# Row factors of a norm sent round through DRAM instead of transposed, and two small edits in a two-layer trunk

## Chip, cores, metric

One core of one Trainium2 chip. The metric is the device time in microseconds (us) of one execution of the whole program; less is better.

## What is computed

The program is a trunk of two layers for one sequence of 512 tokens and 1024 features, all in float32. Layer 0 has a gated linear attention as its mixer, layer 1 a sparse attention (compressed, selected and window keys) whose keys and values, shared, are projected from the normed residual stream. Each layer adds attention to a memory and a feed-forward part with a convolution of width 3. A norm of all rows ends it.

```python
def rmsnorm(x, g):
    y = x * lax.rsqrt(jnp.mean(x * x, axis=-1, keepdims=True) + EPS)
    return y * g

h = x
for i in range(DEPTH):                                  # DEPTH = 2
    if i == N_A_LAYERS:                                 # before layer 1
        shared = shared_kv(h, kv_norm, w_kv_shared, ...)   # rmsnorm(h, kv_norm) @ w_kv, then compressed keys
    xn = rmsnorm(h, norm_mix[i])
    mem_kv = rmsnorm(mem, norm_mem[i]) @ w_mem_kv[i]
    ...                                                 # main = gla_mixer(...) in layer 0, nsa_mixer(...) in layer 1
    mo = mem_attention(mq, mem_kv)
    h = h + jnp.concatenate([main, mo], axis=-1) @ w_out[i]
    h = h + conv_ffn(rmsnorm(h, norm_ffn[i]), w_up[i], conv_w[i], conv_b[i], w_down[i])
return rmsnorm(h, final_norm)
```

## The kernel before

The residual stream is held transposed, as eight tiles `h[k]` of 128 features by 512 tokens. Every float32 product is made from three matmuls of halves: ACT writes the high half of an operand, rounded to the type float32r, DVE subtracts it to get the low half (`split_to`, `wget`), and TensorE adds high x high, low x high, high x low. Weights come as 512 KB tiles `wraw` from DRAM, issued by SP.

A framework schedules the instructions and sets the semaphores; each engine then runs its own list in order. The helper `after(a, b)` fixes that `a` stands behind `b` in an engine's list or in the schedule without a semaphore. Tiles with a tag share a fixed number of buffers, so a new tile waits for the last reader of the old one.

The change touches three places.

*The norm of layer 1's mixer.* A norm is applied late: the products are made with the unnormed stream and their results are multiplied by one factor per token. `rms_sums` adds up the squares with matmuls against a column of ones; the result `rc` has tokens on the partitions (128 x 4), DVE scales it, and POOL raises it to the power -1/2. But the products here have features on the partitions and tokens along the row, so the factors are needed in each partition, as `rb` (128 x 512). `rms_rows` does that with four transposes of a broadcast column (L351, TensorE) into a bank of PSUM and one copy by ACT (L353). In `nsa_layer` the loop over the eight feature tiles makes the product with the compressed keys' and values' weights (L1566, into four banks `pk`); at its step 3 it calls `rms_sums`, at step 5 `rms_rows`. After the loop come the gates' products (L1571), then `kf = pk[f] * rb` on DVE (L1575), which empties the banks for the next keys (L1605). Sixteen copies on SP's queue stack `kf` into `T` (L1578, L1579); DVE adds positions to it (`tp`, L1653) and TensorE multiplies that (L1666).

*The last steps of the sparse attention.* Twelve steps (`steps`, six pairs of heads, two sets of query tiles each) run as a pipeline: scores of the next step (`scores`, with L1761 on DVE, L1763 on ACT, L1768 and L1771 on POOL), transposes of this step's weights (`weights_t`: TensorE L1706, then copies PT by ACT or DVE, L1873), products with the values of an earlier one (`values`). After steps 8, 9 and 10 the outputs `o[0]`, `o[1]`, `o[2]` of the first three pairs are split into halves for the output product `w_out` (L942); PcT is the transposed weights of the compressed part (copy L1805).

*The last rows of the program.* In `ffn_seven` the function `end` finishes two of four blocks of 128 tokens behind the last matmuls; here tokens are on the partitions. `closing` adds the last product to the rows (`plus`, L1378), takes the sum of their squares on ACT (L1383) and multiplies them by the final gain on DVE (L1384). `factor` (L1387, DVE) scales that sum and adds the part known earlier (`pre`), `rooted` (L1391, POOL) raises it to -1/2, `closed` (L1397, L1399) multiplies the rows and sends them out.

Of the kernel before, what the change touches and what calls it, by code (L numbers as in the profile page):

```python
# [12 lines left out]
F32 = mybir.dt.float32  # L13
FR = mybir.dt.float32r
AF = mybir.ActivationFunctionType
ALU = mybir.AluOpType
AX = mybir.AxisListType

S = 512
D = 1024  # L20
# [154 lines left out]
class Trunk:  # L175
# [102 lines left out]
    def split_to(self, hi, lo, src, scale=None):  # L278

        nc = self.nc  # L280
        if scale is None:
            self.high_ins = nc.scalar.activation(hi, src, AF.Copy)  # L282
            nc.vector.tensor_tensor(out=lo, in0=src, in1=hi.bitcast(F32), op=ALU.subtract)  # L283
        else:
            self.high_ins = nc.scalar.activation(hi, src, AF.Copy, scale=scale)
            nc.vector.scalar_tensor_tensor(out=lo, in0=src, scalar=scale, in1=hi.bitcast(F32), op0=ALU.mult, op1=ALU.subtract)
# [60 lines left out]
    def rms_rows(self, N, tag):  # L347

        pb = self.ps("pt")
        for t in range(N // 128):  # L350
            self.nc.tensor.transpose(pb[:, 128 * t:128 * t + 128], self.rc[:, t:t + 1].to_broadcast([128, 128]), self.ident)  # L351
        self.rb = self.t(self.tmp if not tag else self.mpool, [128, N], "rb" + tag, bufs=1)
        self.nc.scalar.copy(self.rb, pb[:, :N])  # L353

    def rms_at(self, first, second, N=S, tag=""):
        return {first: lambda: self.rms_sums(N, tag), second: lambda: self.rms_rows(N, tag)}
# [858 lines left out]
    def ffn_seven(self, l):  # L1215


        nc, tc, T = self.nc, self.tc, NJ // 2
# [108 lines left out]
        def end(mms):  # L1327
# [52 lines left out]
            def closing(t, c, a, bank=None):  # L1380
                plus(t, c, banks[2][t] if bank is None else bank)
                jk = self.t(self.tmp, [128, 512], "rb", bufs=1)
                nc.scalar.activation(jk[:, c], y[t][0][:, c], AF.Square, accum_out=a)  # L1383
                dve(nc.vector.tensor_tensor(out=z[t][:, c], in0=y[t][0][:, c], in1=gb[0][:, c], op=ALU.mult))  # L1384

            def factor(t, a, r):
# [25 lines left out]
            plus(1, cs[1], banks[2][1])  # L1412
            closed(0)
            factor(1, ss[:, 5, 0:1], pre[:, 1:2])
            closing(1, cs[1], ss[:, 1, 0:1], own)
            factor(1, ss[:, 1, 0:1], rc[:, 1:2])
            rooted(1)
            closed(1)

# [93 lines left out]
    def nsa_layer(self):  # L1513
        nc, I, tc = self.nc, self.I, self.tc
        GKV, GMIX = 6, 1
        with ExitStack() as outer:
# [17 lines left out]
            with tc.tile_pool(name="nsap", bufs=2) as pp:  # L1534
# [19 lines left out]
                for n, k in enumerate(order):  # L1554
                    if n % 2 == 0:
                        wh, wl = self.wget(self.W["kvc"][k // 2], GKV, (k, k + 1))
                    if n == 3:
                        self.rms_sums(S, "")
                    if n == 5:
                        self.rms_rows(S, "")  # L1560
                        gate_weights()
                    xh, xl = self.x[k]
                    for f in range(4):
                        ws = slice(512 * (k % 2) + 128 * f, 512 * (k % 2) + 128 * f + 128)
                        for i, (u, w_) in enumerate(((wh, xh), (wl, xh), (wh, xl))):
                            nc.tensor.matmul(pk[f], u[:, ws], w_, start=n + i == 0, stop=n == 7 and i == 2)  # L1566
# [207 lines left out]
            def compressed(a):  # L1774
# [27 lines left out]
                pt = self.ps("pt")  # L1802
                for u in range(2):
                    tr(pt[:, 128 * u:128 * u + 128], Pc[:, 2 * u:2 * u + 2], self.ident)
                nc.scalar.copy(PcTs[a % 2], pt[:, :256].rearrange("p (u t) -> p u t", u=2))  # L1805
                yield

            run = lambda g, n=1: [next(g, None) for _ in range(n)]
# [46 lines left out]
            with tc.tile_pool(name="nsac", bufs=2) as cp:  # L1855
# [3 lines left out]
                def weights_t(s):  # L1859

                    a, qts = steps[s]
                    for hh in range(2):
                        for qt in qts:
                            n = 128 * (qt + 1)
                            P = Ps.pop((a, qt, hh))
                            PT = PTs[a, qt, hh] = self.t(cp, [128, 2, n], f"PT{qt}")
                            for brs in ((0, 1),) if qt < 2 else ((0,), (1,)):
                                pt = self.ps("acc" if brs == (1,) and s < 8 else "pt")
                                for j, br in enumerate(brs):
                                    for kt in range(qt + 1):  # L1870
                                        tr(pt[:, n * j + 128 * kt:n * j + 128 * kt + 128], P[:, br, 128 * kt:128 * kt + 128], self.ident)
                                eng = nc.vector.tensor_copy if qt == 1 or qt == 3 and brs[0] else nc.scalar.copy
                                ins = eng(PT[:, brs[0]:brs[-1] + 1, :], pt[:, :n * len(brs)].rearrange("p (b k) -> p b k", b=len(brs)))  # L1873
                                if qt != 1 and not (qt == 3 and brs[0]):
                                    turned[s] = ins
                                yield

                def values(*ss):
# [25 lines left out]
                for s, (a, qts) in enumerate(steps):  # L1904
# [7 lines left out]
                    for i in range(6):  # L1912
# [13 lines left out]
                        if i == 0 and s < 11:  # L1926
                            run(before, 4)
                        run(now)
                        run(proj, 2)
                        if qts[0] == 0 and i in (0, 5):  # L1930
                            run(c)
                        if i == 2 and s == 11:
                            run(before, 2)
                    if 8 <= s < 11:
                        main[s - 8] = self.split(o[s - 8], self.xp, [128, S], "x")
                run(values(11), 2)
            self.w_out(1, main)
# [26 lines left out]
```

## Time and profile before

| | us |
|---|---|
| median of 3 runs | 1230.78 |
| lowest, highest | 1229.76, 1231.19 |
| profiled execution, whole | 1230.46 |
| its span, first to last instruction | 1228.6 |

In the profile PE is TensorE's matmul, PEld its loading of weights (which overlaps), DVE VectorE, ACT ScalarE, POOL GpSimd and SP SyncE, the engine that issues most DMAs. L12 is line 12 of the kernel. A row of the timeline has start (us from the span's start), length, engine, line, operation, out<-in by tile names, the count of merged instructions, and in brackets the idle time before it with what ended it. A row that ends in two or more merged instructions gives the length of all of them. Matmuls overlap, so the distance between their starts tells more than their length. A row of an instruction's group has its shortest, median and longest duration in ns. In the table of DMAs the last number is us from issue to landing; a queue's row has packets, MB, and the share that its packets took of 16 DMA engines over the span. In a row by stretch come the bounds, the length, the busy time of PE, PEld, DVE, ACT and POOL, the granted TensorE clock (1.00 is full), the DMA engines' busy share and GB/s.

### The profile page before, as it was taken

To read this page: it belongs to the slowest core of one execution; us is meant where nothing else is said; L and a number is where in the kernel's file an instruction comes from. 1 tells how busy PE (TensorE), PEld (TensorE's weight loads), DVE (VectorE), ACT (ScalarE), POOL (GpSimd) and SP (SyncE) were. 2 spreads that over 40 slices of the span, in tenths; PEclk is the share of its full clock that TensorE was granted. 3 is DMA by queue.
4 is the path that set the end of the run, shared out by engine and by line. 5 is a ranking of instruction groups with operands and counts; after the bars stand their busy time and mean duration, and the time that the engine had idled before them with its cause. 6 is when DMAs were issued, how large, how long until landed. Compare 5 with 4: busy or idle time off the path is not lost.

```text
span 1228.6 us, 19292 instructions
## 1 busy us (share of the span) xinstructions
PE 1219.9 (99%) x7189; PEld 1037.3 (84%) x7189; DVE 929.3 (76%) x1714; ACT 667.1 (54%) x1276; POOL 131.1 (11%) x179
## 2 busy tenths in 40 slices
PE   9999999999999999999999999999999999999997
PEld 7888888888888888899888788888888888888886
DVE  7775887599777767878768677974698777777785
ACT  7666555455444444456535777773555444444564
POOL 1000121000000000000103265660000000000000
PEclk9999999999999999999999999999999999999999
DMA  7422111324343343453736333312234334343533
GB/s 260 125 90 77 53 37 46 120 81 150 121 130 112 120 136 105 139 166 99 216 114 205 87 82 95 112 40 69 86 120 138 119 120 133 109 137 120 165 110 112
DMA packets 49594, 142.94 MB, mean 116 GB/s; under 512 B 5679, under 2 KB 9296, under 8 KB 49500
## 3 DMA queue, kind: packets, MB, share of 16 engines
q1 hardware_dynamic: 47692, 139.19, 36.8%
q10 hardware_dynamic: 1808, 2.51, 0.7%
q8 instruction: 57, 0.93, 0.3%
q14 instruction: 37, 0.30, 0.1%
HBM read 133.77 MB, written 2.15 MB: 111 GB/s over the span
## 4 chain that ended last, share of the span: by engine, by line
PE 96%; DVE 1%; ACT 1%; DMA 0%; issue 0%; POOL 0%; SPq 0%; ACTq 0%; POOLq 0%; DVEq 0%
PE acc L979 38%; PE acc L942 5%; PE acc L304 4%; PE acc L693 4%; PE po L1705 3%; PE po L322 3%; PE acc L1705 3%; PE po L1040 3%; PE sc L1040 3%; PE acc L1040 3%; PE sc L1236 2%; PE po L1236 2%; PE acc L1236 2%; PE acc L322 2%; PE sc L304 2%; PE pt L1706 2%
## 5 line engine op out<-in xcount | busy, mean ns | idle before, releaser
L979 PE MATMUL acc<-xh,wl 128*128 128x512 f32 x688 | 267.9, 389 | 0.0
L979 PE MATMUL acc<-xh,wh 128*128 128x512 f32 x688 | 267.8, 389 | 0.0
L979 PE MATMUL acc<-xl,wh 128*128 128x512 f32 x688 | 267.6, 389 | 0.0
L268 ACT ACTIVATE wh<-wraw 128x1024 fp32r<-128x1024 f32 x138 | 145.7, 1056 | 95.8 <-PE acc L942 30.0
L269 DVE TENSOR_TENSOR wl<-wraw,wh 128x1024 fp32r<-128x1024 f32 x138 | 171.7, 1244 | 23.5 <-ACT wh L268 22.8
L979 PEld LDWEIGHTS acc<-xl,wh 128*128 128x128 f32 x688 | 129.1, 188 | 26.9
L979 PEld LDWEIGHTS acc<-xh,wh 128*128 128x128 f32 x688 | 129.2, 188 | 26.4
L979 PEld LDWEIGHTS acc<-xh,wl 128*128 128x128 f32 x688 | 129.1, 188 | 26.1
L965 DVE SCALAR_TENSOR_TENSOR hc<-acc,h,hc 128x511 f32<-128x511 f32 (+1 forms) x144 | 107.3, 747 | 54.4 <-ACT hc L963 53.1
L963 ACT ACTIVATE hc<-acc,h 128x512 f32<-128x512 f32 x72 | 56.0, 777 | 116.8 <-PE acc L979 116.7
L283 DVE TENSOR_TENSOR wl<-wraw,wh 128x1024 fp32r<-128x1024 f32 (+3 forms) x61 | 69.2, 1139 | 16.3 <-ACT wh L282 16.1
L282 ACT ACTIVATE wh<-wraw 128x1024 fp32r<-128x1024 f32 (+3 forms) x61 | 59.0, 970 | 26.7 <-DMA wraw<-in_wp 8.4
L1771 POOL TENSOR_TENSOR P<-P,ssm 128x256 f32<-128x256 f32 (+3 forms) x48 | 63.4, 1343 | 1.9
L1763 ACT ACTIVATE P<-P,smn 128x128 f32<-128x128 f32 (+3 forms) x96 | 53.3, 557 | 10.1 <-DVE smn L1761 8.4
L1761 DVE CUSTOM_DVE_ANT_0 P<-sc,strip 128x128 f32<-128x128 f32 (+3 forms) x72 | 30.0, 434 | 9.5 <-PE sc L1705 9.3
L1525 POOL MEMSET kcz<- 128x128 f32 x1 | 0.2, 210 | 341.7 <-PE acc L1040 341.7
L1025 DVE TENSOR_TENSOR wraw<-wraw,wraw 128x512 f32<-128x512 f32 x22 | 15.1, 688 | 28.4 <-DMA wraw<-in_wp 28.4
L1292 POOL TENSOR_TENSOR yrc<-yrc,mhalf 128x2 f32<-128x2 f32 x1 | 0.7, 698 | 330.0 <-DVE yrc L1291 330.0
L1449 ACT ACTIVATE hc<-hc 128x512 f32<-128x512 f32 x22 | 13.9, 633 | 34.3 <-DVE hc L965 34.1
L1705 PE MATMUL po<-PT,V 128*64 128x128 f32 x480 | 30.3, 273 | 0.0
L1706 PE MATMUL pt<-ident,P 128*128 128x128 f32 x184 | 29.5, 275 | 0.1
L360 DVE TENSOR_TENSOR h<-acc,h 128x512 f32<-128x512 f32 x14 | 9.7, 690 | 25.8 <-PE acc L942 20.5
(594 smaller groups left out, 3140.9 us busy)
## 6 DMA issues: line engine op xcount, KB each, us to landing
wraw<-in_wp SPq DMA_DIRECT2D x227, 512.0 KB, 3.7
strip<-vecd SPq DMA_DIRECT2D x12, 448.0 KB, 3.5
qd<-qf SPq DMA_DIRECT2D x24, 128.0 KB, 2.7
wraw<-in_wp SPq DMA_DIRECT2D x8, 256.0 KB, 3.5
mt<-in_memT SPq DMA_DIRECT2D x16, 128.0 KB, 3.1
h<-in_xp SPq DMA_DIRECT2D x2, 512.0 KB, 6.1
T<-kf SPq DMA_DIRECT2D x8, 128.0 KB, 2.3
T<-kf SPq DMA_DIRECT2D x8, 127.8 KB, 2.4
```

The source lines that it names most:

```text
L268: self.split_ins = nc.scalar.activation(wh, raw, AF.Copy)
L269: self.low_ins = nc.vector.tensor_tensor(out=wl, in0=raw, in1=wh.bitcast(F32), op=ALU.subtract)
L283: nc.vector.tensor_tensor(out=lo, in0=src, in1=hi.bitcast(F32), op=ALU.subtract)
L304: self.nc.tensor.matmul(ps[:M, :N], u[:, M * k:M * k + M], x[k][i][:, :N], start=n == 0, stop=n == 23)
L322: nc.tensor.matmul(ps[:, :N], s_, m_, start=k == 0 and n == 0, stop=k == KC - 1 and n == 2)
L942: nc.tensor.matmul(banks[m], a[:, o], b, start=k == 6 and i == 0, stop=k == 5 and i == 2)
L965: nc.vector.scalar_tensor_tensor(out=dst[:, i:], in0=u[:, :S - i], scalar=tap(2 - i), in1=dst[:, i:], op0=ALU.mult, op1=ALU.add)
L979: pe(nc.tensor.matmul(pu[half], a[:, o], self.x[k][b], start=k == 0 and n == 0, stop=k == KC - 1 and n == 2))
L1040: pe(nc.tensor.matmul(dst, a[:, o], b, start=first and n == 0 and i % 2 == 0, stop=stop and n == 2, skip_group_check=True))
L1236: pe(nc.tensor.matmul(bank[i][:, c], a[:, ts], b[:, c], start=first and n == 0, stop=stop and n == 2, skip_group_check=True))
L1705: mm = lambda *args, **kw: pe(nc.tensor.matmul(*args, **kw))
L1771: nc.gpsimd.tensor_tensor(out=P, in0=P, in1=f[:, i, :].unsqueeze(2).to_broadcast([128, 2, 128 * t + 128]), op=ALU.mult)
```

## The change

`rms_spread` takes the place of `rms_sums` and `rms_rows` for the norm of layer 1's mixer: the 128 x 4 factors are written to DRAM as one row of 512 (512 pieces of 4 bytes), then read back into all 128 partitions. Both DMAs are issued by POOL. The other edits move the split of `o[2]` into step 11 with a fixed place, and let DVE take the last sum of squares, its scale and the addition of `pre` in one instruction, written straight into `rc`.

```diff
+    def rms_spread(self, eng):
+
+        self.rms_sums(S, "")
+        d = self.t(self.dram, [S // 128, 128], "rcd")
+        eng.dma_start(d.rearrange("t p -> p t"), self.rc)
+        self.rb = self.t(self.tmp, [128, S], "rb", bufs=1)
+        eng.dma_start(self.rb, bass.AP(tensor=d.tensor, offset=d.offset, ap=[[0, 128], [1, S]]))
...
             def closing(t, c, a, bank=None):
                 plus(t, c, banks[2][t] if bank is None else bank)
                 jk = self.t(self.tmp, [128, 512], "rb", bufs=1)
-                nc.scalar.activation(jk[:, c], y[t][0][:, c], AF.Square, accum_out=a)
+                if bank is None:
+                    nc.scalar.activation(jk[:, c], y[t][0][:, c], AF.Square, accum_out=a)
+                else:
+                    dve(nc.vector.tensor_tensor_reduce(out=jk[:, c], in0=y[t][0][:, c], in1=y[t][0][:, c], scale=1.0 / D, scalar=pre[:, 1:2],
+                                                       op0=ALU.mult, op1=ALU.add, accum_out=a))
                 dve(nc.vector.tensor_tensor(out=z[t][:, c], in0=y[t][0][:, c], in1=gb[0][:, c], op=ALU.mult))
...
             factor(1, ss[:, 5, 0:1], pre[:, 1:2])
-            closing(1, cs[1], ss[:, 1, 0:1], own)
-            factor(1, ss[:, 1, 0:1], rc[:, 1:2])
+            closing(1, cs[1], rc[:, 1:2], own)
             rooted(1)
...
                     if n == 3:
-                        self.rms_sums(S, "")
+                        self.rms_spread(nc.gpsimd)
                     if n == 5:
-                        self.rms_rows(S, "")
                         gate_weights()
...
-                nc.scalar.copy(PcTs[a % 2], pt[:, :256].rearrange("p (u t) -> p u t", u=2))
+                turned[13] = nc.scalar.copy(PcTs[a % 2], pt[:, :256].rearrange("p (u t) -> p u t", u=2))
...
                                     turned[s] = ins
+                                elif s == 11:
+                                    turned.setdefault(12, ins)
...
                         run(now)
+                        if s == 11 and i == 0:
+                            main[2] = self.split(o[2], self.xp, [128, S], "x")
+                            after(self.high_ins, turned[13])
+                            after(self.low_half, turned[12])
                         run(proj, 2)
...
-                    if 8 <= s < 11:
+                    if 8 <= s < 10:
                         main[s - 8] = self.split(o[s - 8], self.xp, [128, S], "x")
```

The line numbers of the kernel after are some 8 to 16 higher. TensorE's list loses four transposes and is otherwise the same, SP's is the same. At the norm POOL's list reads as follows, with each instruction's waits, before (wgl is the gates' weights, rc the factors, rcm those of the memory's norm):

```order
L1550 COPY fold_5944<-ident_93 36x36 [waits Pool_49]
L1550 COPY fold_5944<-ident_93 36x36
L1543 TENSOR_TENSOR wgl_5942<-wgl_5942,h_81 128x288 [waits DMAHW5_49,Pool_49]
L345 TENSOR_TENSOR rc_6006<-rc_6006,mhalf_109 128x4 [waits DVE_49]
L345 TENSOR_TENSOR rcm_6443<-rcm_6443,mhalf_109 128x2 [waits DVE_49]
```

and after, where rcd is the row in DRAM and DMASW the semaphores of POOL's own DMAs:

```order
L1561 COPY fold_5944<-ident_93 36x36
L1554 TENSOR_TENSOR wgl_5942<-wgl_5942,h_81 128x288 [waits DMAHW5_49,Pool_49]
L345 TENSOR_TENSOR rc_6006<-rc_6006,mhalf_109 128x4 [waits DVE_49]
L359 DMA rcd_6009<-rc_6006 128x4x1 [waits Pool_49]
L361 DMA rb_6011<-rcd_6009 128x512 [waits DMASW0_49]
L345 TENSOR_TENSOR rcm_6440<-rcm_6440,mhalf_109 128x2 [waits DVE_49]
```

The two DMAs stand directly behind the factors, the second waits for the first to land, and DVE's first kf<-acc now waits for the second one and for TensorE.

At the end of the attention, DVE's list before (P are the last scores, ssm their sums, PT the transposed weights, xl the low half of an output, o[2] or, from po, a later one):

```order
L1761 ISA P_1593_8804,smn_8805<-po_8818,strip_8537 128x384
L1761 ISA smn_8805 128x1
L1873 COPY PT_1596_8811<-pt_8827 128x512
L283 TENSOR_TENSOR xl_8838<-o_1213_7252,xh_8837 128x512
L1765 RECIPROCAL ssm_8789<-ssm_8789 128x4
L1873 COPY PT_1603_8841<-pt_8842 128x512
L1873 COPY PT_1609_8884<-pt_8885 128x512
```

and after:

```order
L1771 ISA P_1593_8801,smn_8802<-po_8815,strip_8534 128x384
L1771 ISA smn_8802 128x1
L1883 COPY PT_1596_8808<-pt_8824 128x512
L1775 RECIPROCAL ssm_8786<-ssm_8786 128x4
L1883 COPY PT_1601_8834<-pt_8835 128x512
L283 TENSOR_TENSOR xl_8842<-o_1213_7249,xh_8841 128x512
L1883 COPY PT_1609_8881<-pt_8882 128x512
```

The low half of o[2] has moved behind the reciprocal and one copy; on ACT its high half has moved from ahead of the last six score instructions to behind the copy of PcT.

The last instructions of DVE before (xh the rows, sq the rows times the gain, yss the sums of squares, ypre the part known earlier, yrc the factor):

```order
L1387 SCALAR_TENSOR_TENSOR ypre_9246<-yss_9245,ypre_9246 128x1
L1378 TENSOR_TENSOR xh_11560<-po_11984,xh_11560 128x256
L1384 TENSOR_TENSOR sq_11983<-xh_11560,xh_11442 128x256
L1387 SCALAR_TENSOR_TENSOR yrc_9247<-yss_9245,ypre_9246 128x1
L1397 TENSOR_SCALAR sq_11983<-sq_11983,yrc_9247 128x256 x2
```

and after:

```order
L1399 SCALAR_TENSOR_TENSOR ypre_9243<-yss_9242,ypre_9243 128x1
L1386 TENSOR_TENSOR xh_11557<-po_11981,xh_11557 128x256
L1394 ISA rb_12046,yrc_9244<-xh_11557,ypre_9243 128x256
L1394 ISA yrc_9244 128x1
L1396 TENSOR_TENSOR sq_11980<-xh_11557,xh_11439 128x256
L1409 TENSOR_SCALAR sq_11980<-sq_11980,yrc_9244 128x256 x2
```

The reduction and the reading of its accumulator stand ahead of the product with the gain, and the factor needs nothing from ACT.

More of the change, by code (lines that the diff above doesn't have):

```diff
@@ L282, in split_to @@
             self.high_ins = nc.scalar.activation(hi, src, AF.Copy)
-            nc.vector.tensor_tensor(out=lo, in0=src, in1=hi.bitcast(F32), op=ALU.subtract)
+            self.low_half = nc.vector.tensor_tensor(out=lo, in0=src, in1=hi.bitcast(F32), op=ALU.subtract)
         else:
```

## Prediction

> **What bounds the kernel now.** I read the page first: busy time of each engine, then the chain that ended last. Both name TensorE.
>
> ```profile
> PE 1219.9 (99%) x7189; PEld 1037.3 (84%) x7189; DVE 929.3 (76%) x1714; ACT 667.1 (54%) x1276; POOL 131.1 (11%) x179
> PE 96%; DVE 1%; ACT 1%; DMA 0%; issue 0%; POOL 0%; SPq 0%; ACTq 0%; POOLq 0%; DVEq 0%
> ```
>
> TensorE works 1219.9 us of a span of 1228.6 us. So an edit pays only if it takes matmuls away, closes a gap between them, or shortens what follows the last one. It costs if it opens a gap. Each of the three edits is therefore read in the timeline of its own place.
>
> **The norm's row factors.** The next rows are the timeline, in order of time, from the factors (POOL, L345) to the first products that hang on them.
>
> ```profile
> 594.04 1.02 POOL L345 TENSOR_TENSOR rc<-rc,mhalf 128x4 f32<-128x4 f32 x1 [4.97 <-DVE rc L344]
> 598.75 0.39 PE L1566 MATMUL po<-xh,wl 128*128 128x512 f32 x1
> 598.98 0.39 PE L1566 MATMUL po<-xl,wh 128*128 128x512 f32 x1
> 599.20 0.60 PE L351 MATMUL pt<-ident,rc 128*128 128x128 f32 x4
> 599.56 0.48 PE L1566 MATMUL acc<-xh,wh 128*128 128x512 f32 x1
> 599.88 0.40 PE L1566 MATMUL acc<-xh,wl 128*128 128x512 f32 x1
> 600.69 0.57 ACT L353 COPY rb<-pt 128x512 f32<-128x512 f32 x1
> 606.22 1.28 DVE L1575 TENSOR_TENSOR kf<-acc,rb 128x512 f32<-128x512 f32 x2
> 615.36 3.74 DVE L1653 TENSOR_TENSOR tp<-T,h 128x1024 f32<-128x1024 f32 x2
> 618.29 0.46 PE L1666 MATMUL sc<-tp,mo0h 128*128 128x124 f32 x2
> ```
>
> Removed: four transposes and ACT's copy. Matmuls start 0.23 us apart (598.75, 598.98). From 598.98 to 599.88 there are two such steps and the transposes: 0.90 us, of which 0.90 - 2 x 0.23 = 0.44 is theirs. **TensorE gains 0.44 us.** The copy (0.57) lies on ACT, which is off the chain; I cost it at nothing.
>
> Added: two DMAs on POOL's own queue, the second of which waits for the first (the order shows the wait). Nothing urgent of POOL's stands behind them (its next instruction is the same power for the memory's norm), and SP's and ACT's queues keep their order, so the DMAs are not put ahead of another queue's loads; they share the 16 DMA engines with them. The new wait is DVE's: kf<-acc now needs the DMA. Behind it on DVE stand the low halves of the next weights and, through SP's sixteen T<-kf copies, tp. Who waits last is TensorE's first product with tp. In the rows above the first tp ends at 615.36 + 3.74/2 = 617.23 and that product starts at 618.29, 1.06 later; with about 0.1 for the signal, kf may be late by some 0.9. The copies T<-kf go out one by one as kf comes, so I carry a delay of kf through one to one. Freed of the transposes, kf can start at 606.22 - 0.44 = 605.78. **So the round trip costs nothing if rb lands by 605.78 + 0.9 = 606.7**, 11.6 us after the factors are there (594.04 + 1.02 = 595.06); each us beyond costs one.
>
> No POOL DMA and no write of 4-byte pieces is in the trace, so I bound them by these rows: landings of small DMAs, packets per queue, the DMA engines' share around the place, one issue.
>
> ```profile
> out<-xl ACTq DMA_DIRECT2D x1, 256.0 KB, 2.0
> cmask<-in_c_cmask ACTq DMA_DIRECT2D x1, 16.0 KB, 3.5
> b<-in_cb ACTq DMA_DIRECT2D x1, 32.0 KB, 4.7
> xh<-in_fg ACTq DMA_DIRECT2D x2, 256.0 KB, 3.9
> q1 hardware_dynamic: 47692, 139.19, 36.8%
> q10 hardware_dynamic: 1808, 2.51, 0.7%
> 595.00:601.00 6.00, 6.00 (x30) 4.96 (x29) 4.22 (x12) 5.07 (x14) 0.05 (x1) 1.00 0.52 160
> 601.00:607.00 6.00, 6.00 (x28) 4.93 (x27) 4.71 (x13) 4.50 (x12) 0.00 (x0) 1.00 0.56 180
> 606.93 0.52 SPq L1578 DMA_DIRECT2D T<-kf  x1
> ```
>
> Low end: each of the two lands like the quickest 256 KB write, 2.0, with no issue time: 595.06 + 4.0 = 599.1. Middle: the write like cmask (128 short rows, 3.5), the read like in_fg (the same spread of one row over 128 partitions, 3.9), an issue of 0.5 each: 8.4, rb at 603.5. High end: both as slow as in_cb (4.7), an issue of 0.5 each, and the write's 512 single elements, 32 to an engine, as packets of their own. A packet takes 0.7% x 16 x 1228.6 / 1808 = 76 ns on q10 and 152 ns on q1 (36.8% over 47692); at 152 that is 4.9 more, rb at 595.06 + 10.4 + 4.9 = 610.4, late by 3.7. I take the middle: cmask and in_fg have these shapes, and the engines are only half taken (0.52, 0.56). It leaves 3.2 us, so the cost is 0; the range keeps 0 to 3.7. The gain of 0.44 has an end of 0 where a later wait that the change leaves swallows the lead.
>
> [...]
>
> **The split of o[2], moved one step later.** On ACT it goes behind the copy of PcT, on DVE behind the reciprocal and one PT copy. The timeline of before there:
>
> ```profile
> 819.23 0.65 ACT L282 ACTIVATE xh<-o 128x512 fp32r<-128x512 f32 x1
> 820.51 0.62 ACT L1763 ACTIVATE P<-P,smn 128x384 f32<-128x384 f32 x1
> 822.39 2.47 POOL L1771 TENSOR_TENSOR P<-P,ssm 128x512 f32<-128x512 f32 x2
> 823.65 0.20 PEld L1706 LDWEIGHTS pt<-ident,Pc 128*128 128x128 f32 x2 [0.50 <-POOL P L1771]
> 823.82 1.58 DVE L283 TENSOR_TENSOR xl<-o,xh 128x512 fp32r<-128x512 f32 x1
> 824.40 0.60 PE L1706 MATMUL pt<-ident,P 128*128 128x128 f32 x4
> 824.56 0.19 ACT L1763 ACTIVATION_READ_ACCUMULATOR P<-P,smn 128x1 f32 x1
> 825.41 0.66 DVE L1873 COPY PT<-pt 128x512 f32<-128x512 f32 x1
> 825.89 0.48 ACT L1873 COPY PT<-pt 128x384 f32<-128x384 f32 x1 [0.88 <-PE pt L1706]
> 826.12 0.31 PEld L1706 LDWEIGHTS pt<-ident,P 128*128 128x128 f32 x3 [0.40 <-DVE PT L1873]
> ```
>
> TensorE waits 0.40 at 826.12 for the PT copy of 825.41, which stood behind the 1.58 us of xl<-o. Its transposes were done at 824.40 + 0.60 = 825.00. Without xl ahead, and with the reciprocal placed after the sums (824.56 + 0.19 = 824.75, some 0.2 long), the copy starts near 825.05, 0.36 earlier. **Gain 0.3**, ends 0 and 0.90: the upper end adds the 0.50 at 823.65, which hangs on ACT's row before it. I don't count that one, because ACT's work from 820.51 on starts only when DVE delivers, so the 0.65 taken out at 819.23 becomes idle time there. In its new place xh<-o fills the 0.88 that ACT idles before 825.89, and xl keeps nobody waiting: TensorE's first products with it stand behind the attention's last ones in the order.
>
> **The last sum of squares.** It goes from ACT to DVE, with the scale and the partial sum taken along. Timeline of the end, then a DVE reduction of the same kind and width from the attention, then one pair of rows in which POOL's power meets a DVE instruction:
>
> ```profile
> 1222.33 0.42 DVE L1378 TENSOR_TENSOR xh<-po,xh 128x256 f32<-128x256 f32 x1
> 1222.78 0.42 DVE L1384 TENSOR_TENSOR sq<-xh,xh 128x256 f32<-128x256 f32 x1
> 1223.63 0.56 POOL L1391 TENSOR_TENSOR yrc<-yrc,mhalf 128x1 f32<-128x1 f32 x1 [2.62 <-DVE yrc L1387]
> 1224.22 0.72 ACT L1399 ACTIVATE xh<-xh,yrc 128x512 f32<-128x512 f32 x1 [0.86 <-POOL yrc L1391]
> 821.39 0.42 DVE L1761 CUSTOM_DVE_ANT_0 P<-sc,strip 128x256 f32<-128x256 f32 x1
> 821.73 0.09 DVE L1761 DVE_READ_ACCUMULATOR2_ANT smn<- 128x1 f32 x1
> L345 POOL TENSOR_TENSOR rcm<-rcm,mhalf x2: 697/1220/1742, 49.4 to 640.4; 128x2 f32<-128x2 f32 x2
> 49.30 1.23 DVE L269 TENSOR_TENSOR wl<-wraw,wh 128x1024 fp32r<-128x1024 f32 x1
> 49.35 1.74 POOL L345 TENSOR_TENSOR rcm<-rcm,mhalf 128x2 f32<-128x2 f32 x1 [23.53 <-DVE rcm L344]
> ```
>
> The reduction starts where the product sq started, 1222.78, and its accumulator is read 0.34 to 0.43 later, at 1223.21; the power could start at 1223.28 instead of 1223.63, a gain of 0.35. But sq now follows the reduction on DVE at about 1223.2, ahead of the power. In the last two rows the same power on two columns began 0.05 after a DVE instruction with two SBUF inputs and took 1.74, against 0.70 alone; it ended 0.56 after DVE did, 0.14 less than its own length. So the power of 0.56 would end 0.42 after sq (1223.2 + 0.42): 1224.04 against 1224.19. **Gain 0.1**, ends 0 and 0.35; I take the row in which the two collide, since the order puts sq ahead.
>
> [...]
>
> **Sum:** 0.44 + 0.3 + 0.1 = 0.84 us less. The profiled execution took 1230.46 (span 1228.6 and 1.86 around it), so 1229.6 for such a one; the median of the runs is 1230.78, 0.32 above it, which gives **1229.9 us**. The three runs lie 1.43 apart, so 0.2% (2.5 us) is about what can be told from no change.
>
> **The rivals.** (1) The round trip is late and a DMA wait takes the place of the transposes. Its place is kf<-acc, it decides from 606.7 on, and it makes the kernel slower than before from 606.7 + 0.84 = 607.5. At the high end it gives 1229.9 + 3.7 = 1233.6; over 0.2% slower needs rb past 610.0. For it: two transfers in a row, 512 tiny writes, and loads on all engines. Against it: 3.2 us of room in the middle case. [...]
> (2) All gains reach their upper ends: 0.44 + 0.90 + 0.35 = 1.69, 1229.1. For it: the 0.50 at 823.65 is a true wait. Against it: the collision above.
> (3) The change doesn't do what it says: the freed 0.44 turns into a wait further on, since TensorE later needs weights from loads of their own pace, and the small edits give nothing: 1230.8. Against it: the chain is TensorE's at 96%.
>
> **How the numbers follow.** Forecast 0.60; rival 1 0.22, half of it past 610.0; rival 2 0.08; rival 3 0.10. The range reaches down to rival 2 less half of the runs' distance, 1229.1 - 0.7 = 1228.4, and up to where rb lands at 610.0, 1229.9 + 3.3 = 1233.2. Slower by over 0.2%: the late half of rival 1 and a little for what bounds don't cover, 0.14. Faster by over 0.2% lies past every upper end; 0.05. The rest, 0.81, is within 0.2%.
>
> **What would show it.** No gap in TensorE near 599, and kf<-acc waiting for TensorE and not for a DMA: the round trip is hidden. A DVE wait on a POOL DMA there, then a gap before L1666's successor: rival 1. The wait before the last transposes at 826 gone: the second term; the power at the end starting late or long although its input is there: the collision. The forecast is wrong if two POOL transfers take over 15 us, or if the new queue adds time outside the span, of which this trace shows nothing.

## The result and the profile after

The changed kernel is slower: 1237.21 us (median of 4 runs, 1236.40 to 1238.28) against 1230.42 for the kernel before beside it (1229.76 to 1231.19); the ratio is 1.0056, 95% interval 1.0043 to 1.0069. That is 6.8 us against a forecast of 0.84 less, and past the range's upper end of 1233.2. The profiled execution has a span of 1236.0 us, 7.4 longer than that of before.

From the page of the changed kernel, the engines' busy time and the chain that ended last by engine:

```profile
PE 1222.4 (99%) x7185; PEld 1039.4 (84%) x7185; DVE 928.0 (75%) x1715; ACT 665.4 (54%) x1273; POOL 132.7 (11%) x181
PE 94%; DMA 3%; DVE 1%; ACT 1%; issue 0%; POOL 0%; SPq 0%; POOLq 0%; DVEq 0%; ACTq 0%
```

DMA has gone from 0% of the chain to 3%. The busy total hides the loss: TensorE is "busy" 2.5 us longer although it has four transposes fewer, a first sign that some products ran slower. The place is the round trip. POOL's timeline, with the two issues, then the landings of three kinds of DMA that were issued between 594 and 613 us (count, KB each, median us from issue to landing), then the row of POOL's DMA queue from 595 to 599 us (its share is that of the 4 us):

```profile
595.63 0.98 POOL L359 DMA_DIRECT2D rcd<-rc  x1 [0.31 <-POOL rc L345]
605.84 0.58 POOL L361 DMA_DIRECT2D rb<-rcd  x1 [9.23 <-DMA rcd<-rc]
...
mt<-in_memT SPq DMA_DIRECT2D x5, 128.0 KB, 10.8
rb<-rcd POOLq DMA_DIRECT2D x1, 256.0 KB, 5.8
rcd<-rc POOLq DMA_DIRECT2D x1, 2.0 KB, 9.9
...
q0 software_dynamic: 32, 0.00, 4.6%
```

The write of 2 KB took 9.9 us and the read 5.8, so rb was there at about 611.6, 5 us past the 606.7 that the prediction allowed. And something stands here that the prediction did not look for: mt, the rows of the memory, loaded by SP, landed 10.8 us after their issue, where the page of before has a median of 3.1 us (2.2 in the same window). The write itself is 32 packets on POOL's queue, all of them before 599 us; 4.6% of 4 us is 0.18 us of each DMA engine. The other 6 us until its landing at 605.5 are not in its packets, and what it waits for there the profile does not show. Timeline of the engines that take mt and then kf, and the two waits that TensorE has as a result:

```profile
605.80 0.42 ACT L333 ACTIVATE sqm<-mt 128x256 f32<-128x256 f32 x1 [6.32 <-DMA mt<-in_memT]
606.25 0.43 DVE L334 TENSOR_TENSOR sqaccm<-sqaccm,sqm 128x256 f32<-128x256 f32 x1 [6.21 <-ACT sqm L333]
613.66 1.28 DVE L1585 TENSOR_TENSOR kf<-acc,rb 128x512 f32<-128x512 f32 x2
614.49 0.47 PE L1615 MATMUL acc<-xh,wh 128*128 128x512 f32 x1 [2.99 <-DVE kf L1585]
624.57 0.48 PE L1676 MATMUL sc<-tp,mo0h 128*128 128x124 f32 x2 [1.50 <-DVE tp L1663]
```

kf starts at 613.66 (before: 606.22), with no idle time of DVE ahead of it. rb had been there for 2 us: kf stood in DVE's list behind the sums and low halves of the late mt. Then the granted clock, by windows of 6 us (window, length, busy time of PE, PEld, DVE, ACT and POOL, granted clock, DMA share, GB/s):

```profile
601.00:607.00 6.00, 6.00 (x28) 4.95 (x28) 0.75 (x2) 0.82 (x2) 0.58 (x1) 1.00 0.44 22
613.00:619.00 6.00, 4.51 (x13) 3.60 (x14) 4.86 (x12) 2.48 (x7) 0.00 (x0) 0.72 0.65 183
625.00:631.00 6.00, 6.00 (x27) 5.16 (x26) 1.48 (x2) 1.61 (x4) 0.00 (x0) 0.72 0.57 149
```

Between 601 and 607 us, most of which the write takes, the DMA engines move 22 GB/s (before: 180 in the same window). After each of TensorE's two waits the clock falls to 0.72 over 6 us, as these products show: they start 0.43 us apart until 618.15, and 0.23 apart from 618.45 on. The last three rows are for the account below: tp in the changed kernel, then a later product with tp in it and in the kernel before.

```profile
615.16 0.63 PE L1615 MATMUL acc<-xl,wh 128*128 128x512 f32 x1
615.59 0.63 PE L1615 MATMUL acc<-xh,wh 128*128 128x512 f32 x1
...
618.45 0.40 PE L1615 MATMUL acc<-xh,wl 128*128 128x512 f32 x1
618.68 0.39 PE L1615 MATMUL acc<-xl,wh 128*128 128x512 f32 x1
...
622.65 3.69 DVE L1663 TENSOR_TENSOR tp<-T,h 128x1024 f32<-128x1024 f32 x2
631.76 0.38 PE L1676 MATMUL sc<-tp,mo1h 128*128 128x124 f32 x2
623.89 0.38 PE L1666 MATMUL sc<-tp,mo1h 128*128 128x124 f32 x2
```

The account, by the starts of the same products in the two profiles: TensorE is 624.57 - 618.29 = 6.28 us behind at its first product with tp, 631.76 - 623.89 = 7.87 a little later, and 7.60 at the end of the attention (831.25 against 823.65, row below). The nine products from 614.49 to 618.15 took 3.66 in place of 9 x 0.23 = 2.07, so the first fall slowed them by 1.59. By these rows that cost nothing in the end: the first tp was ready at 622.65 + 3.69/2 = 624.50, behind kf and the copies T<-kf, and TensorE would have stood there 1.59 longer. The second fall has no such wait behind it; the 7.87 - 6.28 = 1.59 are its price. So 6.28 come from the late kf, and 1.59 from the clock.

### The profile page after: what moved, and what is told of

Its sections match the earlier page's. It is cut to its first block, busy times and chain, and to the rows that moved or that the text cites. A ratio compares the mean times of both kernels' runs of the same rounds, so it can differ in the third digit from the quotient of the medians.

```text
span 1236.0 us, 19286 instructions
## 1 busy us (share of the span) xinstructions
PE 1222.4 (99%) x7185; PEld 1039.4 (84%) x7185; DVE 928.0 (75%) x1715; ACT 665.4 (54%) x1273; POOL 132.7 (11%) x181
## 4 chain that ended last, share of the span: by engine, by line
PE 94%; DMA 3%; DVE 1%; ACT 1%; issue 0%; POOL 0%; SPq 0%; POOLq 0%; DVEq 0%; ACTq 0%
PE acc L987 38%; PE acc L950 5%; PE po L1715 4%; PE acc L701 4%; PE acc L304 4%; PE po L322 3%; PE acc L1715 3%; PE po L1048 2%; PE acc L1048 2%; PE sc L1048 2%; PE sc L1244 2%; PE po L1244 2%; PE acc L322 2%; PE acc L1244 2%; PE pt L1716 2%; PE sc L304 2%
## 5 line engine op out<-in xcount | busy, mean ns | idle before, releaser
L1773 ACT ACTIVATE P<-P,smn 128x128 f32<-128x128 f32 (+3 forms) x96 | 53.3, 557 | 10.2 <-DVE smn L1771 8.6
```

## The experiments

Three theories stood at the start. **Theory 1**: the write holds up SP's loads of mt, and DVE's list, taken in order, passes that on to kf. **Theory 2**: only the factors themselves are late. **Theory 3**, beside either: TensorE's clock falls because TensorE stood still, and the price of a wait rises by that. All times are medians, and ratios are against the kernel before on the same chip.

**The small edits alone.** Edit to the changed kernel:

```diff
-                        self.rms_spread(nc.gpsimd)
+                        self.rms_sums(S, "")
                     if n == 5:
+                        self.rms_rows(S, "")
```

> The two small edits alone: the factors go back to four transposes and ScalarE's copy, the split of o[2] and the last sum of squares stay as changed. If the round trip through DRAM is the whole loss, the time is before minus 0.3 (the wait ahead of the last transposes) minus 0.15 (the closing chain), 0.45 us less: 1230.0 where before is 1230.4. If the moved split costs something outside the window in which it was looked for, 1230.4 or more. The changed kernel's loss of 6.8 us must not be seen at all; 1234 or more would put a part of it on the small edits.

Measured: 1230.08 us, ratio 0.9998 (0.9989 to 1.0007). The loss is all the round trip's. The expected 0.45 lies inside the interval and is not shown by the times.

**The round trip issued, and nothing reads it.** The transposes make rb again; the read goes to a spare tile:

```diff
-        self.rb = self.t(self.tmp, [128, S], "rb", bufs=1)
-        eng.dma_start(self.rb, bass.AP(
+        spare = self.t(self.sparepool, [128, S], "spare", bufs=1)
+        eng.dma_start(spare, bass.AP(
...
                     if n == 5:
+                        self.rms_rows(S, "")
```

> The factors come from the transposes, as before, and the same two POOL transfers are issued besides, the write of rc and the broadcast read, into a tile that nothing reads. Theory 1 (the write holds up the other loads): mt lands as late as in the changed kernel, ScalarE waits about 6 us for it, VectorE's list stands behind it, and kf with it: first kf product at 611 to 614, time 1233.5 to 1237. Theory 2 (only the late factors matter): kf starts at about 606, time 1229.9 to 1230.5, and mt's landings are those of before (median 3.1 us).

Measured: 1235.97 us, ratio 1.0045 (1.0033 to 1.0058). Timeline and landings of this kernel:

```profile
604.97 0.42 ACT L333 ACTIVATE sqm<-mt 128x256 f32<-128x256 f32 x1 [3.94 <-DMA mt<-in_memT]
606.64 0.57 ACT L353 COPY rb<-pt 128x512 f32<-128x512 f32 x1
611.11 1.28 DVE L1587 TENSOR_TENSOR kf<-acc,rb 128x512 f32<-128x512 f32 x2
...
rcd<-rc POOLq DMA_DIRECT2D x1, 2.0 KB, 8.2
```

No wait of the kernel is on these two DMAs, and 5.5 of the 6.8 us are there all the same. Theory 2 as the whole falls. Even the copy that makes rb (before: 600.69) is 6 us late, because it stands behind the late mt on ScalarE.

**Rows of 16 bytes.** The write keeps each partition's four factors together; the readers of rb take a view that puts the order right.

```diff
-        eng.dma_start(d.rearrange("t p -> p t"), self.rc)
+        eng.dma_start(d, self.rc)            # d: 128 rows of 4
...
-nc.vector.tensor_tensor(out=kf, in0=pk[f], in1=rb, op=ALU.mult)
+nc.vector.tensor_tensor(out=pt_(kf), in0=pt_(pk[f]), in1=tp_(rb), op=ALU.mult)
```

> The write puts each partition's four factors side by side in DRAM (128 rows of 16 bytes in place of 512 pieces of 4 bytes), the read stays a 2 KB row spread over 128 partitions, and the four VectorE readers take rb through a view that puts the order right. If the 512 pieces make the write slow, it takes about 3 us (before's small POOL transfers), mt is not held up, rb lands at about 604 to 606, and the time is 1229.9 to 1231. If the price is that of the queue that POOL issues to, whatever the pieces, the write stays near 10 us and the time near 1237. In between (5 us): rb at 608, kf 2 us late, about 1233.

Measured: 1234.27 us, ratio 1.0034 (1.0022 to 1.0045).

```profile
rcd<-rc POOLq DMA_DIRECT2D x1, 2.0 KB, 3.2
...
605.76 0.42 ACT L333 ACTIVATE sqm<-mt 128x256 f32<-128x256 f32 x1 [1.34 <-DMA mt<-in_memT]
607.74 2.05 DVE L1588 TENSOR_TENSOR kf<-acc,rb 128x512 f32<-128x512 f32 x2
```

The write took 3.2 us, so POOL's queue as such is not slow. (The expectation names small POOL transfers of the kernel before; that kernel has none, and its small DMAs are those shown in the prediction, of 2.0 to 4.7 us.) The time is a miss by 3 us: two kf took 2.05 us in place of 1.28 through the view, a cost of the experiment that the expectation left out, and mt still made ScalarE wait 1.34. The profile shows both but does not split the 3.8 us between them.

**Work where TensorE waits.** Thirteen products of 128x512 into a bank that nothing reads, ahead of the wait for kf:

```diff
+                spin(13)
                 gt = self.t(pp, [100, S], "gt", bufs=1)
```

> The changed kernel with 13 products of 128x512 into a bank that nothing reads, put where TensorE waits 3.0 us for kf (13 x 0.23 us = 3.0). The plan of some later VectorE and ScalarE rows shifts with them. Theory 3 (the granted clock falls because TensorE stood still): no fall to 0.72 between 613 and 619 us, products after the wait 0.23 us apart instead of 0.43, time 1.5 to 1.8 us less than the changed kernel, about 1235.5, although work was added. If the fall has another cause, the clock is 0.72 there as before, and the time is 1237.2 or more.

Measured: 1234.88 us, ratio 1.0035 (1.0023 to 1.0047). Windows of this kernel:

```profile
613.00:619.00 6.00, 6.00 (x28) 4.96 (x27) 2.74 (x6) 0.00 (x0) 0.00 (x0) 1.00 0.80 187
619.00:625.00 6.00, 5.59 (x34) 4.86 (x33) 4.45 (x4) 0.29 (x1) 0.00 (x0) 1.00 0.91 218
```

The clock stays at 1.00, with a TensorE wait of 0.41 us left in place of 2.99 and 1.50, so the fall goes with the waits. It does not follow every one: in the kernel with the rows of 16 bytes TensorE waits 1.33 us, in the one with the write alone (below) first 2.16 us, and the clock stays at 1.00 behind both. The time proves less: kf came at 610.85 in this profile, not at 613.66, so the loads were held up less, and later rows had moved. The fair partner is the kernel before this one with unread transfers, kf at 611.11: it waits 3.12 us and its clock falls to 0.78 between 619 and 625; it took 1235.97, 1.1 us more than this one with 3 us of useless products. The intervals of the two overlap.

**Loads of mt ahead of the write.**

```diff
-            mt = self.t(pool, [128, MEM], "mt", bufs=3)
+            mt = self.t(pool, [128, MEM], "mt", bufs=8)
```

> The changed kernel with eight buffers in place of three for the memory rows mt, so that their loads go out ahead of the write of rc; the plan of some VectorE and ScalarE rows on mt shifts with it. Theory 1 (the held-up loads set kf's start): mt has landed before 601, ScalarE waits for no late mt, and what is left is the factors' own lateness, rb at 607 to 611 against the 606.7 that is needed: time 1230 to 1234, most of the 6.8 us gone if rb is near 607. Theory 2 (the factors' own lateness is the whole): 1236.5 to 1237.5, as in the changed kernel.

Measured: 1235.12 us (1231.87 to 1237.86), ratio 1.0037 (1.0024 to 1.0050), past the 1230 to 1234 of theory 1 and short of theory 2.

```profile
609.92 1.29 DVE L1585 TENSOR_TENSOR kf<-acc,rb 128x512 f32<-128x512 f32 x2 [1.54 <-DMA rb<-rcd]
621.68 0.79 PE L1676 MATMUL sc<-tp,mo0h 128*128 128x124 f32 x2 [3.94 <-DVE tp L1663]
```

Here kf does wait for rb, 1.54 us, and starts 3.7 us later than before. Neither cause needs the other: each alone makes kf late, and taking one away leaves most of the price. ScalarE still waits 2.71 us for one late mt, at 604.70, so the separation is not clean.

**Rows of 512 bytes.** One transpose makes four rows of rc; everything else is the changed kernel's round trip.

```diff
+        pb = self.ps("pt")
+        self.nc.tensor.transpose(pb[:4, :128], self.rc, self.ident)
+        rt = self.t(self.sparepool, [4, 128], "rt", bufs=1)
+        self.nc.scalar.copy(rt, pb[:4, :128])
-        eng.dma_start(d.rearrange("t p -> p t"), self.rc)
+        eng.dma_start(d, rt)
```

> One TensorE transpose turns rc from 128x4 to 4x128, and ScalarE copies it; the write is then 4 rows of 512 bytes, and the broadcast read is that of the changed kernel, so that no reader of rb needs another order. If the pieces of 4 bytes are the price: the write takes 2 to 3.5 us from about 598.5, rb lands at 605 to 607, mt is not held up, and the time is 1230 to 1231.5. If the 128-partition read holds mt up too, mt's median stays at 3.5 or more, as with the rows of 16 bytes, and the time is 1232 or more.

Measured: 1229.75 us (1229.51 to 1230.43), ratio 0.9996 (0.9988 to 1.0005).

```profile
600.93 0.59 POOL L364 DMA_DIRECT2D rb<-rcd  x1 [1.57 <-DMA rcd<-rt]
...
rb<-rcd POOLq DMA_DIRECT2D x1, 256.0 KB, 4.6
rcd<-rt POOLq DMA_DIRECT2D x1, 2.0 KB, 2.0
```

The same 2 KB by the same queue in 2.0 us, rb at about 605.5, kf at 607.03, no wait of TensorE there. The broadcast read stands among the same loads of mt, and they landed in 3.3 us (median), so the read holds nothing up that costs time. This is the version to keep if the round trip is wanted: about 7.4 us faster than the change (0.9996 against 1.0056), and not to be told from the kernel before.

**SP's hardware queue.** `self.rms_spread(nc.gpsimd)` becomes `self.rms_spread(nc.sync)`.

> The same write of 512 pieces and the same read, issued by SP to its hardware queue in place of POOL's; the write stands ahead of three loads of mt there and the read behind them. If the slowness belongs to POOL's queue, the write takes about 3 us and the time is 1230 to 1232. If it belongs to 512 pieces of 4 bytes on whatever queue, the write takes 8 us or more, the mt loads behind it on the same queue land 8 us or more after their issue, and the time is 1237 or more.

Measured: 1236.13 us, ratio 1.0048 (1.0035 to 1.0061). SP's timeline:

```profile
595.33 0.38 SPq L359 DMA_DIRECT2D rcd<-rc  x1
603.70 0.33 SPq L361 DMA_DIRECT2D rb<-rcd  x1
```

The read, which waits for the write, goes out 8.4 us after it. The queue is not the cause. The time is 0.9 us under the expectation, and the mt loads landed in 5.8 us, not 8.

**A quarter of the pieces.**

```diff
-        eng.dma_start(d.rearrange("t p -> p t"), self.rc)
+        eng.dma_start(d[0:1].rearrange("t p -> p t"), self.rc[:, 0:1])
```

> Only the first column of rc is written, 128 pieces of 4 bytes in place of 512, and the read repeats it four times, so that the factors of three quarters of the tokens are those of the first quarter (the output differs by that). If the write's time goes with the number of pieces, it is about 3.2 us, what 128 rows of 16 bytes took, and the time is 1230 to 1232. If it goes with pieces under some size and not with their number, it stays at 8 to 10 us.

Measured: 1239.27 us, ratio 1.0069 (1.0054 to 1.0083). Landings:

```profile
rb<-rcd POOLq DMA_DIRECT2D x1, 256.0 KB, 9.7
rcd<-rc POOLq DMA_DIRECT2D x1, 0.5 KB, 8.7
```

128 pieces of 4 bytes take 8.7 us, 128 pieces of 16 bytes about 3: the number of pieces is not the price. The time itself can't be used, since the read in four parts took 9.7 us in place of 5.8.

**The write alone, side by side and 64 bytes apart.** With queue and number out, a fourth theory was left: pieces that lie side by side in DRAM wait for one another. Both kernels leave the read out and make rb by transposes; the second also has:

```diff
-        d = self.t(self.dram, [S // 128, 128], "rcd")
-        eng.dma_start(d.rearrange("t p -> p t"), self.rc)
+        d = self.t(self.dram, [S // 128, 128, 16], "rcd")
+        eng.dma_start(d[:, :, 0:1].rearrange("t p c -> p t c"), self.rc.unsqueeze(2))
```

> The factors come from the transposes; of the two transfers only the write of rc in 512 pieces of 4 bytes is issued, and nothing reads what it writes. The unread write and read together cost 5.5 us. If the write alone holds up the loads of mt, most of that stays: write 7.5 to 10 us, ScalarE's wait for mt near 604 about 4 us, time 1234 to 1236. If the read does it, the time is 1230 to 1231.

> The same write alone, its 512 pieces of 4 bytes now 64 bytes apart in DRAM in place of side by side; factors from the transposes. A quarter of the pieces took as long as all, so the price is not their number. If it is that neighbouring pieces share a stretch of DRAM, the write takes 3 to 4 us and the time is 1230 to 1231. If it is the piece's size of 4 bytes, the write takes 7.5 to 10 us and the time is 1234 to 1236, as with the write side by side.

Measured, side by side: 1237.83 us, ratio 1.0058 (1.0045 to 1.0071).

From its timeline, with the window behind its first wait, and the landing of the write:

```profile
613.17 1.28 DVE L1584 TENSOR_TENSOR kf<-acc,rb 128x512 f32<-128x512 f32 x2
614.00 0.47 PE L1614 MATMUL acc<-xh,wh 128*128 128x512 f32 x1 [2.16 <-DVE kf L1584]
613.00:619.00 6.00, 5.00 (x22) 4.21 (x23) 4.36 (x10) 1.99 (x5) 0.00 (x0) 1.00 0.72 194
...
rcd<-rc POOLq DMA_DIRECT2D x1, 2.0 KB, 10.2
```

Measured, 64 bytes apart: 1229.94 us, ratio 0.9997 (0.9988 to 1.0006).

```profile
rcd<-rc POOLq DMA_DIRECT2D x1, 2.0 KB, 2.9
```

The time is 1.8 us past the expectation: the write took 10.2 us here and 8.2 in the kernel that also had the read. One write that nothing reads carries the whole loss of the change, and the same 512 pieces of 4 bytes carry none once they lie 64 bytes apart. Neither their size nor their number is the cause, but that they lie side by side.

**The read alone**, from an input, into a spare tile (`src = self.I["memT"][0:2, :]`, the same access pattern).

> Only the broadcast read of 2 KB over 128 partitions is issued, from an input in place of rcd, into a tile that nothing reads; factors from the transposes. If the read alone adds little to mt, as the rows of 512 bytes suggest (mt's median landing 3.3 us), it takes 4 to 4.7 us and the time is 1229.7 to 1230.8. If it holds mt up too, ScalarE waits 1 us or more for mt near 605 and the time is 1232 or more.

Measured: 1229.75 us, ratio 0.9995 (0.9986 to 1.0003); kf starts at 606.43. POOL's timeline:

```profile
585.66 0.76 POOL L360 DMA_DIRECT2D spare<-in_memT  x1
```

This read hangs on nothing, so it went out at 585.66, some 14 to 20 us ahead of the round trip's reads, and was over before the loads that the write held up: between 594 and 613 us POOL's queue moves no packet. The run says only that the read costs nothing there; that it costs nothing in its place is shown by the rows of 512 bytes.

**The slow write in a quiet stretch.** The small edits alone, and behind gates:

```diff
+                    d = self.t(self.dram, [S // 128, 128], "rcd")
+                    nc.gpsimd.dma_start(d.rearrange("t p -> p t"), gates[:, :, 0])
```

> The small edits with the transposes, and a write of 512 pieces of 4 bytes that nothing reads, moved to a stretch with few loads: its source is the first column of gates, ready at about 619.6, and the DMA engines carry 0.33 of their time before 625 and nothing after it. If the pieces are slow by themselves, the write takes 7 us or more there too, and the time stays 1230 to 1231, since no load that is soon needed stands beside it. If they are slow only among other loads, it takes 2 to 4 us.

Measured: 1230.31 us, ratio 1.0000 (0.9991 to 1.0009). Its landing, from an issue at 619.95:

```profile
rcd<-gates POOLq DMA_DIRECT2D x1, 2.0 KB, 9.3
...
625.00:631.00 6.00, 6.00 (x35) 5.15 (x35) 5.88 (x10) 3.14 (x6) 0.00 (x0) 1.00 0.03 1
```

The write is slow by itself, 9.3 us with few loads about, and does no harm where no load is awaited. From 625 us to its landing at 629.25 the DMA engines are idle but for 0.03 of their time: what is slow is not the engines' work on packets.

**Spacings between.** The write alone once more, with `128, 16` replaced by `128, 2`, `128, 4` and `128, 8`.

> The write alone, unread, its 4-byte pieces 8 bytes apart. If pieces that share a 64-byte stretch wait for one another, 8 of them share it here: a write of 5 to 7 us (half way between 10.2 with 16 and 2.9 with 1), mt held up in part, time 1231 to 1235. If only pieces that touch are slow: 2.9 us and 1230.

> The same with 16 bytes between the pieces, 4 in a 64-byte stretch: 3.5 to 5 us and 1230 to 1232 if the sharers wait for one another; 2.9 us and 1230 if only touching pieces are slow; 8 us or more and 1234 or more if any sharing of a stretch is as bad as full sharing.

> The same with 32 bytes between the pieces, 2 in a 64-byte stretch: 3 to 4 us and 1230 to 1230.7 if the sharers wait for one another; 2.9 us and 1230 if only touching pieces are slow; 8 us or more if any sharing of a stretch is as bad as full sharing.

Landing of the write for 8, 16 and 32 bytes in turn, with the eight mt between 590 and 612 us for 8:

```profile
rcd<-rc POOLq DMA_DIRECT2D x1, 2.0 KB, 5.2
mt<-in_memT SPq DMA_DIRECT2D x8, 128.0 KB, 4.8
```

```profile
rcd<-rc POOLq DMA_DIRECT2D x1, 2.0 KB, 2.9
```

```profile
rcd<-rc POOLq DMA_DIRECT2D x1, 2.0 KB, 4.1
```

| bytes from piece to piece | write us | mt us (8 loads) | kf starts | median us | ratio (95%) |
|---|---|---|---|---|---|
| 4 | 10.2 | 7.3 | 613.17 | 1237.83 | 1.0058 (1.0045 to 1.0071) |
| 8 | 5.2 | 4.8 | 608.21 | 1231.47 | 1.0010 (1.0000 to 1.0019) |
| 16 | 2.9 | 3.2 | 606.08 | 1230.10 | 0.9998 (0.9989 to 1.0008) |
| 32 | 4.1 | 2.8 | 607.18 | 1229.90 | 0.9996 (0.9987 to 1.0006) |
| 64 | 2.9 | 2.9 | 606.62 | 1229.94 | 0.9997 (0.9988 to 1.0006) |

Twice the spacing halves the write, down to about 3 us at 16 bytes (one profile each). At 8 bytes no two pieces touch, and the write is still slow; the rows of 16 bytes touch, and took 3.2. So it is not touching that counts but how densely the pieces lie: 10.2, 5.2 and 2.9 us at 4, 8 and 16 bytes. That those in one stretch of DRAM wait for one another is the theory's picture and no trace shows it; nor do the runs say how long such a stretch would be, because the number in it and the spacing changed together. The 4.1 at 32 bytes, one profile, breaks the order without showing in the time.

## Why the prediction was wrong

**The term that failed: the cost of the round trip, 0 with an upper end of 3.7.** It was put together from the landings of cmask (3.5) and in_fg (3.9). The read was sized roughly right (4.1 to 5.8 against 3.9). The write was not: 8.2 to 10.2 us in the kernels that had it, against 3.5. cmask is a read of 128 short rows; I took its shape for the write's and had no row of a write of small neighbouring pieces. The high end did add a price for 512 pieces, 4.9 us, as packets of their own; it came near the write's 9.9 (4.7 + 0.5 + 4.9), but as a price by number, which the quarter refutes, and by packets, of which the write has 32 in all, done 6 us before it lands. It got a small chance.

**The step that failed with it: "they share the 16 DMA engines with them".** I counted the DMAs as late for their own reader only. The unread write shows that they were late for others: with the write alone SP's loads all but stood (22 GB/s from 601 to 607 us, against 180 before), mt came late (9.1 us for those issued between 594 and 613, against 2.2), and DVE's and ScalarE's lists, taken in order, carried that to kf. The prediction named what stood behind kf on DVE, but not what stood ahead of it. That rb was late as well (theory 2, the place of rival 1) is true and by itself nearly enough, as the kernel with eight buffers for mt shows.

**"One to one" held, from kf and not from rb.** rb at 611.6 would have made rival 1's price 611.6 - 606.7 = 4.9 and its time 1234.8. In fact kf started at 613.66, 2 us later, for the mt ahead of it on DVE. By the same rule that is 613.66 - 606.7 = 6.96, less the 0.44 of the transposes 6.52, against the 6.28 by which the first product with tp was late. (The prediction's 0.1 for the signal had no row; here it is 624.57 - 624.50 = 0.07.) The 1.59 of the second fall of the clock come on top, and no step of the prediction had them. The kernel with eight buffers shows the same: kf 3.7 us late, the first product with tp 621.68 - 618.29 = 3.39 late, then a clock of 0.58 in the 6 us from 619 on, 4.9 us by the medians. Rival 1 had the sign and the end of the path, TensorE's product with tp; its sign at the start, a wait of DVE for POOL's DMA ahead of kf, is not in the trace, because the late mt ended after it.

The runs show that small neighbouring pieces are bad (8.2 to 10.2 us) and rows of 512 bytes good (2.0), but 4-byte pieces 64 bytes apart took 2.9 us and held up nothing (mt 2.9), so smallness alone is not the price. What the loads waited for while the slow write ran, at 22 GB/s, no run shows.

**The transposes, 0.44.** Right: TensorE begins the factors' sums 0.27 later than before (593.08 against 592.81) and its last product of the gate logits 0.22 earlier (611.10 against 611.32), 0.49 in all, and no wait stands near 599.

**The split of o[2], 0.3.** Right. The changed kernel's rows, a group of transposes before the place and one behind it:

```profile
831.25 0.20 PEld L1716 LDWEIGHTS pt<-ident,Pc 128*128 128x128 f32 x2 [0.50 <-POOL P L1781]
833.38 0.34 PEld L1716 LDWEIGHTS pt<-ident,P 128*128 128x128 f32 x3
836.65 0.75 PEld L1716 LDWEIGHTS pt<-ident,P 128*128 128x128 f32 x7 [0.17 <-issue]
```

In the second of these rows the wait of 0.40 is gone, in the first the 0.50 that I did not count is still there, and TensorE's lag falls from 831.25 - 823.65 = 7.60 to 836.65 - 829.37 = 7.28, a gain of 0.32. (829.37 is where the same seven start in the timeline of before.)

**The last sum of squares, 0.1.** Right, with the collision:

```profile
1229.78 0.42 DVE L1386 TENSOR_TENSOR xh<-po,xh 128x256 f32<-128x256 f32 x1
1230.24 0.48 DVE L1394 CUSTOM_DVE_ANT_0 rb<-xh,ypre 128x256 f32<-128x256 f32 x1
1230.82 0.67 POOL L1403 TENSOR_TENSOR yrc<-yrc,mhalf 128x1 f32<-128x1 f32 x1 [2.35 <-DVE yrc L1394]
1231.52 0.72 ACT L1411 ACTIVATE xh<-xh,yrc 128x512 f32<-128x512 f32 x1 [1.90 <-POOL yrc L1403]
```

The lag falls from 1229.78 - 1222.33 = 7.45 to 1231.52 - 1224.22 = 7.30, a gain of 0.15. The power took 0.67 beside sq (DVE, from 1230.65 on), not 0.56, and ended 0.42 after sq, as forecast. Six of the experiments make the factors by the transposes and have the two small edits and nothing that holds up a load; their profiled spans are 1228.0 to 1228.2, against 1228.6 of before. Taken one by one their times can't be told from nothing. Taken together, their 63 runs are 0.41 us faster on average than the 69 of the kernel before on the same three chips (95% interval 0.22 to 0.61, chip by chip). That fits the 0.4 predicted for both; the times don't split it between the two, and five of the six carry an idle DMA besides.

## What to carry to other kernels

Before a column is sent to DRAM, look at which bytes neighbouring pieces write: turn it into whole rows first (2.0 us here, against 9.9), or space the pieces out (2.9 to 4.1 from 16 bytes on). Price a new DMA not only for its reader: ask which loads are in flight beside it, and what stands ahead of the critical row in the list of the engine that takes them. And where a wait would open on TensorE, add what its clock may cost behind it, and ask whether a later wait swallows that: here the last wait cost 1.6 us more than its length, the first nothing.

## What the runs showed of the hardware

- 512 writes of 4 bytes side by side took 8.2 to 10.2 us, by POOL's queue or (8.4 from issue to issue) SP's, with loads about or few (9.3); 16 bytes apart or more, 2.9 to 4.1; rows of 16 bytes side by side, 3.2. In the changed kernel the 32 packets of the write were done before 599 us, over 6 us ahead of its landing at 605.5.
- While such a write ran, loads of another queue all but stood: 22 GB/s in place of 180 in the changed kernel, mt's landing 10.8 us in place of 2.2. Where they stood is not shown; the DMA engines' share was 0.44 in that window, so they were neither idle nor full.
- TensorE's granted clock fell after a wait of 3.0 us in the changed kernel, and after one of 1.5, for 3.7 and about 3.8 us by the pitch of its products (0.43 in place of 0.23). It did not fall after one of 2.16 us in the kernel with the write alone, so the length of a wait does not decide by itself.
- A VectorE product with its factor read through a view of every fourth element (the rows of 16 bytes) took 1.03 us in place of 0.64 (2.05 and 1.28 for two).
